# Spreading 1/rms with a stride-zero column, weight halves by accumulating transfers, twenty fills and new transfer constants in the planner

## The chip, the cores and the metric

One Trainium2 chip, one of its cores. The metric is the device time of one execution in microseconds (us). A core has five engines that run beside each other and wait for each other by semaphores: TensorE (PE, with its weight loads as PEld), VectorE (DVE), ScalarE (ACT), GpSimd (POOL) and SyncE (SP, which here only issues transfers). Each engine works through its own list of instructions strictly in the order in which the program put them there.

## The reference, cut to what matters

Two layers; `x` are 256 latent tokens, `xc` 256 context tokens, 1024 wide, everything in float32. The second layer leaves out the context's later part.

```python
for l in range(2):
    mod = silu(c) @ w_ada[l] + b_ada[l]        # nine vectors: shift, scale, gate, three times
    x = x + 0.5*g1 * swiglu(modulate(rmsnorm(x), sh1, sc1), w1, w3, w2)      # ffn 1, also for xc
    h = modulate(rmsnorm(x), sh2, sc2)
    # mixer: h @ w_in gives q, k, v, g of a retention with 8 heads, the low-rank
    # parts of an attention with 8 heads, and two merge gates
    ret = (silu(g) * groupnorm(retention(q, k, v))) @ w_ret_out
    x = x + g2 * ((sigmoid(gate_ret)*ret + sigmoid(gate_mla)*mla) @ w_o)
    x = x + 0.5*g3 * swiglu(modulate(rmsnorm(x), sh3, sc3), w1, w3, w2)      # ffn 2
return rmsnorm(x, final_norm)
```

`rmsnorm(x)` divides each token by the root of its mean square over the 1024 columns.

## The kernel before

**Layout.** Activations lie transposed: partitions are columns of the model, the free dimension is tokens (512 = 256 latent + 256 context), so x is eight tiles of 128x512. A weight tile of 128x1024 (512 KB) holds eight 128x128 blocks.

**Products in two halves.** TensorE multiplies the rounded type float32r in one pass. A float32 operand a is split into hi = round(a) and lo = a - hi, and a product is three matmuls, hi*hi + lo*hi + hi*lo (`mm3`, line 600). For weights `split_w` (line 562) does it: ACT copies `raw` to `wh`, then DVE subtracts to make `wl`. Transfers land in four `raw` buffers; `wh` and `wl` have four each.

**Norm** (lines 622 to 676). `add` squares a tile on ACT and sums on DVE; `stats` sums over partitions with a matmul against ones, which leaves the mean square of token p in partition p; DVE scales it and POOL takes the power -1/2, giving `rstd` with one column for each 128 tokens. `spread` brings this to a row on every partition: DVE multiplies the identity by each column of rstd (`dg`), and a float32 matmul of ones with dg gives 128x256. There are 19 of these: two each for start, n1, n2, n3 and the two low-rank norms of layer 0, and seven in layer 1.

**Stages.** `start` (line 1482) loads x, takes the first norm, computes the first shift and scale tile by tile (five on TensorE, three on DVE) and the first three pairs of ffn tiles as they arrive. It has 20 warm-up matmuls of ones with ones and `N_KEEP` = 5 more ("fills") of low priority. Then for each layer ffn 1, mixer, ffn 2. An ffn goes in three parts of 6, 8 and 8 hidden tiles: `up` makes a hidden tile G (ACT Silu, three DVE operations in `gate_tile`, line 855), `down` multiplies a part's tiles by w2. Between these, `ada_fill` puts the products for later shifts, scales and gates: DVE multiplies a `raw` tile of w_ada with a row into `junk` and sums it (line 726). In the mixer, eight steps `g_step` (line 1117) with one weight tile each go in turn with the retention's steps.

**Who sets the order.** All operations are recorded first. `Plan.order` (line 249) then simulates them: each engine takes, when free, the ready operation of lowest priority number; costs of operations come from `Engine.cost` (line 403). A transfer on SP costs 475 ns of the issuing engine, and lands at the later of its issue + 1100 ns and the one before it, plus bytes at 400 bytes/ns. The order found there is what each engine's list holds; on the chip nothing is reordered. All recorded instructions carry line 368.

Of the kernel before, what the change touches and what calls it, by code (L numbers as in the profile page):

```python
# [14 lines left out]
AF = mybir.ActivationFunctionType  # L15
# [3 lines left out]
P = 128  # L19
# [21 lines left out]
N_TAIL = 3  # L41
N_WARM = 20
N_PE_ADA = 5
N_KEEP = 5
URGENT = 1000
N_FIRST = 2
N_RQ = (1,3)
# [112 lines left out]
class Node:  # L160


    __slots__ = ("calls", "engine", "cost", "table", "port", "prio", "index", "waits", "after", "bufs", "new", "ready", "start", "end")

    def __init__(self, engine, prio, index):
        self.engine, self.prio, self.index = engine, prio, index
        self.calls, self.cost, self.table, self.port = [], 0.0, None, False
        self.waits, self.after, self.bufs, self.new = set(), [], {}, []
        self.ready, self.start, self.end = 0.0, None, None


class Plan:
# [7 lines left out]
    LONG, FAR, HOLD = 500.0, 1000, HOLD  # L180

    COLD = 7000.0

    def __init__(self, tc):
        self.tc = tc
# [63 lines left out]
    def order(self):  # L249
# [14 lines left out]
        later = {e: [] for e in engines}  # L264
        avail = {e: [] for e in engines}
        stuck = {k: [] for k in self.kinds}
        dma, table, port = 0.0, None, 0.0
        for n in nodes:
            if not left[n]:
                heapq.heappush(later[n.engine], (0.0, n.index, n))  # L270
# [17 lines left out]
        while len(done) < len(nodes):  # L288
# [34 lines left out]
                due[b.kind].remove(b.first)  # L323
            n.start = now
            if e == "SP":
                clock[e] = now + 475.0
                n.end = dma = max(now + 1100.0, dma) + n.cost
            else:
                if n.table not in (None, table):
                    now, table = now + self.TABLE, n.table  # L330
                if n.port:

                    now = max(now, port)
                    port = now + n.cost
                slow = 2.0 if e == "PE" and now < self.COLD else 1.0
                n.end = clock[e] = now + slow * n.cost
# [35 lines left out]
class Engine:  # L372
# [5 lines left out]
    def __getattr__(self, method):  # L378
        call = getattr(self.real, method)

        def record(*args, **kwargs):
            views = [v for v in list(args) + list(kwargs.values()) if isinstance(v, View)]
            out = [v for k in ("out", "accum_out") if isinstance(v := kwargs.get(k), View)]
            if "out" not in kwargs and args and isinstance(args[0], View):
                out.append(args[0])
            reads = [v for v in views if not any(v is o for o in out)]

            table = {AF.Silu: 0, AF.Exp: 1, AF.Tanh: 1}.get(args[2]) if method == "activation" else None
            return self.plan.add(self.name, call, args, kwargs, out, reads, self.cost(method, out, reads, kwargs), table,
                                 self.port(method, out, reads, kwargs))  # L390

        return record

    def port(self, method, out, reads, kwargs):

        if self.name == "POOL":
            return method != "memset"
        if self.name != "DVE" or any(v.buf.kind in ("m", "a") for v in out + reads):
            return False
        big = [v for v in reads if math.prod(v.shape[1:]) > 1]  # L400
        return len(big) > 1 or (method in ("tensor_copy", "tensor_scalar") and math.prod(out[0].shape[1:]) > 8)

    def cost(self, method, out, reads, kwargs):
# [3 lines left out]
        psum = any(v.buf.kind in ("m", "a") for v in out + reads)  # L407
        pointers = sum(isinstance(kwargs.get(k), View) for k in ("bias", "scale", "scalar", "scalar1", "scalar2"))
        if self.name == "SP":
            return big.shape[0] * n * 4 / 400.0  # L410
        if self.name == "PE":
            rows, cols = out[0].shape[0], math.prod(out[0].shape[1:])
            if method == "transpose":
# [8 lines left out]
        if self.name == "ACT":  # L422
            return 0.834 * n + (50.0 if psum else 93.0) + 91.0 * pointers + (96.0 if "accum_out" in kwargs else 0.0)
        if self.name == "POOL":
            if kwargs.get("op") == ALU.pow:
                return 300.0 + 165.0 * n
            if method == "memset":
                return 60.0 + 0.78 * n
            return (300.0 + 0.93 * n if method == "tensor_scalar" else 130.0 + 2.13 * n)
# [7 lines left out]
def kernel(  # L437
# [124 lines left out]
    def split_w(raw, n, kind):  # L562
        if kind == "raw":
            return raw
        if kind == "t":
            hi, lo = Halves(T(dt=F32R), T(dt=F32R)), Halves(T(dt=F32R), T(dt=F32R))
            for i in range(2):
                r = raw[:, i * TOK:(i + 1) * TOK]
                act.copy(out=hi.parts[i], in_=r)
                dve.tensor_tensor(out=lo.parts[i], in0=r, in1=hi.parts[i], op=ALU.subtract)  # L570
        else:
            hi, lo = plan.new("wh", n, F32R), plan.new("wl", n, F32R)
            act.copy(out=hi, in_=raw)
            dve.tensor_tensor(out=lo, in0=raw, in1=hi, op=ALU.subtract)
        return Pair(hi, lo)

    def run_steps():
# [44 lines left out]
    class Norm:  # L622
# [39 lines left out]
        def spread(self, a, n):  # L662

            rstd = self.ms.pop(a)
            dg = U(n)
            for i in range(n // P):
                dve.tensor_scalar(out=dg[:, i * P:(i + 1) * P], in0=ident, scalar1=rstd[:, i:i + 1], scalar2=None, op0=ALU.mult)
            bc = self.bc[a] = PA(n)
            pe.matmul(bc, lhsT=ones, rhs=dg, start=True, stop=True)

        def finish(self, a, n=LAT):
            if a not in self.bc:
# [280 lines left out]
    def mixer(l, nrm_in, nrm_out, full):  # L953
# [485 lines left out]
        for i in range(8):  # L1439
            if i % 2 == 0:  # L1440
                step(ret_state(i // 2))
                step(ret_scores(i // 2))
                if i >= 2:
                    step(ret_out(i // 2 - 1))
            step(g_step(i), W("g", i))
            if i % 2 == 0:
                step(ret_av(i // 2))
                if i < 6:
# [288 lines left out]
```

## Time and profile before

| | |
|---|---|
| three timed runs | median 2145.7 us (2140.36 to 2147.9) |
| the profiled execution | 2144.34 us, its span 2142.6 us |
| mean granted TensorE clock | 0.991 |
| instructions | 29830 |
| data read from HBM | 290.78 MB, 136 GB/s over the span |

The span runs from the first to the last instruction; some 1.7 us of the execution lie around it. The busy time of an engine is the union of its instructions. Matmuls are pipelined and their ends are modelled, so a stretch in which TensorE counts as busy can still hold short waits; a wait shows as idle time in brackets before an instruction, with who ended it.

### The profile page before, as it was taken

What the parts mean: (1) busy time and instruction counts of PE and PEld (TensorE: products, weight loads), DVE (VectorE), ACT (ScalarE), POOL (GpSimd) and SP (SyncE); (2) the same over time, 40 slices, a digit from 0 to 9 for tenths busy, and PEclk for the clock granted to TensorE, in tenths of its full rate; (3) what the DMA queues carried; (4) which work ended last, traced back from release to release, by engine and by line L of the source; (5) the groups of instructions that cost most, each with busy time, mean ns of one, the idle gap of its engine ahead of it and who ended that gap; (6) DMA issues with size and microseconds to landing.
All of it is one profiled execution on the core that took longest, in us unless ns stands there. A gap on an engine that the chain in (4) does not pass through costs nothing.

```text
span 2142.6 us, 29830 instructions
## 1 busy us (share of the span) xinstructions
PE 2112.4 (99%) x11630; PEld 1800.7 (84%) x11630; DVE 1402.9 (65%) x2599; ACT 745.1 (35%) x1225; POOL 150.6 (7%) x172
## 2 busy tenths in 40 slices
PE   9999999999999999999999999999999999999998
PEld 6888788987788888988878898888889879999998
DVE  6898785668679435888755473433337967766665
ACT  4222122476433223422212242221225744344433
POOL 0000000211132000100000010000002112100000
PEclk8999999999999999999999999999999999999999
DMA  8476564221121433466665432333233312474663
GB/s 315 148 219 190 181 189 141 91 84 60 60 70 60 128 112 104 138 199 212 189 187 175 139 119 70 109 97 97 90 98 95 116 60 88 149 264 142 205 187 109
DMA packets 87070, 293.76 MB, mean 137 GB/s; under 512 B 9617, under 2 KB 12817, under 8 KB 86929
## 3 DMA queue, kind: packets, MB, share of 16 engines
q1 hardware_dynamic: 86930, 291.87, 43.6%
q8 instruction: 91, 1.49, 0.3%
q14 instruction: 49, 0.40, 0.1%
HBM read 290.78 MB, written 1.05 MB: 136 GB/s over the span
## 4 chain that ended last, share of the span: by engine, by line
PE 71%; DVE 11%; issue 8%; DMA 7%; POOL 1%; ACT 0%; SPq 0%; POOLq 0%; DVEq 0%; ACTq 0%
PE m L368 66%; DMA raw<-in_w_ada_dram 5%; PE a L368 5%; DVE junk L368 5%; DVE t L368 3%; DVE wl L368 2%; DMA t<-in_w_ada_dram 1%; DVE s L368 1%; DVE u L368 1%; POOL s L368 0%; DMA wh<-in_w_ada_dram 0%; POOL t L368 0%; DVE x L368 0%; ACT t L368 0%; DMA raw<-in_w3a_dram 0%
## 5 line engine op out<-in xcount | busy, mean ns | idle before, releaser
L368 PE MATMUL m<-t,wh 128*128 128x512 f32 (+1 forms) x6248 | 1646.8, 351 | 12.2 <-DVE t L368 11.8
L368 PEld LDWEIGHTS m<-t,wh 128*128 128x128 f32 x6248 | 1092.8, 189 | 180.7 <-DVE t L368 14.9
L368 PE MATMUL m<-t,wl 128*128 128x512 f32 (+1 forms) x3124 | 1086.0, 349 | 0.0
L368 ACT CAST wh<-raw 128x1024 fp32r<-128x1024 f32 (+1 forms) x398 | 409.2, 1029 | 959.3 <-PE m L368 824.6
L368 PEld LDWEIGHTS m<-t,wl 128*128 128x128 f32 x3124 | 589.3, 189 | 82.4
L368 DVE TENSOR_TENSOR wl<-raw,wh 128x1024 fp32r<-128x1024 f32 (+1 forms) x398 | 476.5, 1198 | 259.6 <-ACT wh L368 258.6
L368 DVE SCALAR_TENSOR_TENSOR junk<-raw,crow 128x1024 f32<-128x1024 f32 x220 | 268.8, 1222 | 109.9 <-DMA raw<-in_w_ada_dram 106.6
L368 DVE SCALAR_TENSOR_TENSOR x<-m,mod,x 128x256 f32<-128x256 f32 x192 | 86.3, 479 | 124.4 <-PE m L368 124.1
L368 ACT ACTIVATE t<-m 128x512 f32<-128x512 f32 (+1 forms) x155 | 79.3, 513 | 248.1 <-PE m L368 244.0
L368 DVE TENSOR_TENSOR t<-t,t 128x512 fp32r<-128x512 f32 (+7 forms) x252 | 145.4, 585 | 5.0 <-ACT t L368 2.4
L368 DVE TENSOR_TENSOR t<-t,m 128x512 f32<-128x512 f32 (+1 forms) x91 | 54.3, 597 | 109.2 <-PE m L368 103.7
L368 POOL TENSOR_TENSOR s<-s,mhalf 128x2 f32<-128x2 f32 (+1 forms) x31 | 35.5, 1149 | 1163.4 <-DVE s L368 1163.2
L368 PE MATMUL m<-wh,t 128*128 128x512 f32 x288 | 92.1, 399 | 0.0
L368 PE MATMUL a<-t,t 128*64 128x256 f32 (+3 forms) x512 | 87.2, 351 | 4.8 <-DVE t L368 2.8
L368 PEld LDWEIGHTS a<-t,t 128*128 128x128 f32 (+1 forms) x512 | 66.0, 175 | 22.3 <-ACT t L368 4.9
L368 PE MATMUL m<-t,t 128*128 128x256 f32 (+1 forms) x480 | 76.0, 310 | 0.3 <-DVE t L368 0.3
L368 PEld LDWEIGHTS m<-t,t 128*128 128x128 f32 x480 | 65.2, 191 | 5.5 <-issue 1.2
L368 PEld LDWEIGHTS m<-wh,t 128*128 128x128 f32 x288 | 53.2, 188 | 12.6 <-issue 1.2
L368 ACT CAST t<-t 128x512 fp32r<-128x512 f32 (+4 forms) x112 | 55.9, 526 | 11.5 <-DVE t L368 8.9
L368 PE MATMUL m<-wl,t 128*128 128x512 f32 x144 | 56.9, 395 | 0.0
L368 ACT ACTIVATE t<-u,mod 128x256 fp32r<-128x256 f32 x88 | 39.7, 500 | 28.8 <-DVE u L368 28.8
L368 POOL MEMSET t<- 32x512 f32 x32 | 16.1, 528 | 473.7 <-DVE junk L368 257.3
(105 smaller groups left out, 1045.7 us busy)
## 6 DMA issues: line engine op xcount, KB each, us to landing
raw<-in_w_ada_dram SPq DMA_DIRECT2D x122, 512.0 KB, 4.2
raw<-in_w_m_dram SPq DMA_DIRECT2D x76, 512.0 KB, 3.5
raw<-in_w1b_dram SPq DMA_DIRECT2D x44, 512.0 KB, 3.9
raw<-in_w3b_dram SPq DMA_DIRECT2D x44, 512.0 KB, 3.8
raw<-in_w1a_dram SPq DMA_DIRECT2D x41, 512.0 KB, 3.6
raw<-in_w3a_dram SPq DMA_DIRECT2D x41, 512.0 KB, 3.6
raw<-in_w2a_dram SPq DMA_DIRECT2D x32, 512.0 KB, 3.5
raw<-in_w2b_dram SPq DMA_DIRECT2D x32, 512.0 KB, 3.6
```

Of the source, the lines that this page charges most:

```text
L368: call(*[resolve(v) for v in args], **{k: resolve(v) for k, v in kwargs.items()})
```

## The change

Four edits. `spread` takes the column of rstd itself, read 128 times with stride zero, as the stationary operand, and the identity as the moving one: row m of the result is the sum over k of rstd[k] * ident[k, n], so rstd[n] on all partitions. The multiplications on DVE are gone; there is a matmul for each 128 tokens. For the eight `g` weight tiles of each layer the lower half is made by ACT writing -raw (rounded, so -hi) into `wl` and a transfer issued by POOL that adds raw to it. N_KEEP goes from 5 to 20. The planner's constants for transfers change, and it learns to place transfers on POOL.

```diff
-N_KEEP = 5
+N_KEEP = 20
...
+    FIRST, ISSUE, LATENCY, RATE = 2000.0, 560.0, 2000.0, 380.0
...
-        dma, table, port = 0.0, None, 0.0
+        dma, table, port = self.FIRST, None, 0.0
...
             if e == "SP":
-                clock[e] = now + 475.0
-                n.end = dma = max(now + 1100.0, dma) + n.cost
+                clock[e] = now + self.ISSUE
+                n.end = dma = max(now + self.LATENCY, dma) + n.cost
+            elif n.moved:
+
+                clock[e] = now + n.cost
+                dma = max(now + self.LATENCY, dma) + n.moved
+                n.end = dma + 1800.0
...
+            if self.name == "POOL" and method == "dma_start":
+                node.moved += 1.5 * out[0].shape[0] * math.prod(out[0].shape[1:]) * 4 / 270.0
...
-            return method != "memset"
+            return method not in ("memset", "dma_start")
...
-            return big.shape[0] * n * 4 / 400.0
+            return big.shape[0] * n * 4 / Plan.RATE
...
+            if method == "dma_start":
+                return 870.0
...
             act.copy(out=hi, in_=raw)
-            dve.tensor_tensor(out=lo, in0=raw, in1=hi, op=ALU.subtract)
+            if kind == "d":
+
+                act.activation(lo, raw, AF.Copy, scale=-1.0)
+                pool.dma_start(out=lo, in_=raw, accum_op=ALU.add)
+            else:
+                dve.tensor_tensor(out=lo, in0=raw, in1=hi, op=ALU.subtract)
...
             rstd = self.ms.pop(a)
-            dg = U(n)
-            for i in range(n // P):
-                dve.tensor_scalar(out=dg[:, i * P:(i + 1) * P], in0=ident, scalar1=rstd[:, i:i + 1], scalar2=None, op0=ALU.mult)
             bc = self.bc[a] = PA(n)
-            pe.matmul(bc, lhsT=ones, rhs=dg, start=True, stop=True)
+            with plan.together():
+                for i in range(n // P):
+                    pe.matmul(bc[:, i * P:(i + 1) * P], lhsT=rstd[:, i:i + 1].to_broadcast([P, P]), rhs=ident, start=True,
+                              stop=True)
...
-            step(g_step(i), W("g", i))
+            step(g_step(i), W("g", i, "d"))
```

## Rows read from the trace of the kernel before

**Rows 1.** Page, part 1: busy us (share of the span) and instructions of each engine.

```profile
PE 2112.4 (99%) x11630; PEld 1800.7 (84%) x11630; DVE 1402.9 (65%) x2599; ACT 745.1 (35%) x1225; POOL 150.6 (7%) x172
```

**Rows 2.** Windows: length, busy us of PE, PEld, DVE, ACT, POOL, clock, DMA share, GB/s.

```profile
228.00:240.00 12.00, 7.31 (x22) 5.07 (x21) 9.34 (x15) 1.05 (x1) 0.00 (x0) 0.72 0.61 194
1080.00:1092.00 12.00, 9.71 (x34) 7.14 (x34) 7.61 (x15) 1.45 (x2) 0.00 (x0) 0.86 0.72 217
1812.00:1836.00 24.00, 18.20 (x126) 17.03 (x125) 21.27 (x55) 9.31 (x20) 5.88 (x7) 0.86 0.22 67
```

**Rows 3.** Timeline at 226 to 234 us: start, us, what, idle before.

```profile
226.45 1.46 SPq L368 DMA_DIRECT2D raw<-in_w_ada_dram  x2
...
229.90 1.23 DVE L368 SCALAR_TENSOR_TENSOR junk<-raw,crow 128x1024 f32<-128x1024 f32 x1 [1.98 <-DMA raw<-in_w_ada_dram]
...
231.05 0.68 DVE L368 TENSOR_TENSOR t<-t,m 128x512 f32<-128x512 f32 x1
...
233.25 0.79 PE L368 MATMUL m<-t,wh 128*128 128x512 f32 x1 [4.17 <-DVE t L368]
```

**Rows 4.** Timeline of DVE before 1080 us.

```profile
1078.82 1.23 DVE L368 SCALAR_TENSOR_TENSOR junk<-raw,crow 128x1024 f32<-128x1024 f32 x1 [3.14 <-DMA raw<-in_w_ada_dram]
```

**Rows 5.** Waits of DVE: us in total, times, longest.

```profile
DVE junk L368 <- DMA raw<-in_w_ada_dram: 106.6, 57, 4.0
```

**Rows 6.** Page, part 6: issues, KB each, us to landing.

```profile
raw<-in_w_ada_dram SPq DMA_DIRECT2D x122, 512.0 KB, 4.2
raw<-in_w_m_dram SPq DMA_DIRECT2D x76, 512.0 KB, 3.5
```

**Rows 7.** Windows, same columns: layer 1's retention.

```profile
1800.00:1812.00 12.00, 12.00 (x106) 12.00 (x105) 11.39 (x33) 7.25 (x16) 5.77 (x7) 1.00 0.18 68
```

**Rows 8.** Timeline of DVE and PE in layer 1's retention.

```profile
1766.27 1.22 DVE L368 TENSOR_TENSOR wl<-raw,wh 128x1024 fp32r<-128x1024 f32 x1 [5.09 <-ACT wh L368]
...
1812.87 1.23 DVE L368 TENSOR_TENSOR wl<-raw,wh 128x1024 fp32r<-128x1024 f32 x1
1814.01 0.41 DVE L368 SCALAR_TENSOR_TENSOR t<-t,m 128x256 f32<-128x256 f32 x1
...
1814.48 0.39 PE L368 MATMUL m<-t,wh 128*128 128x256 f32 x1 [1.45 <-DVE t L368]
```

**Rows 9.** Timeline at the last norm, 2134 to 2137 us.

```profile
2134.27 0.69 POOL L368 TENSOR_TENSOR s<-s,mhalf 128x2 f32<-128x2 f32 x1 [184.76 <-DVE s L368]
2135.00 0.48 DVE L368 TENSOR_SCALAR u<-ident,s 128x128 f32<-128x128 f32 x2 [0.81 <-POOL s L368]
...
2135.63 0.69 PE L368 MATMUL a<-u,ones 128*128 128x256 f32 x2 [1.64 <-DVE u L368]
```

**Rows 10.** Timeline from 888 to 899 us: the norm ahead of ffn 2, layer 0.

```profile
888.41 1.61 POOL L368 TENSOR_TENSOR s<-s,mhalf 128x2 f32<-128x2 f32 x1 [0.43 <-DVE s L368]
...
890.05 0.95 DVE L368 TENSOR_SCALAR u<-ident,s 128x128 f32<-128x128 f32 x2 [0.19 <-POOL s L368]
...
898.06 0.38 PE L368 MATMUL m<-t,wh 128*128 128x256 f32 x1 [2.10 <-DVE t L368]
```

**Rows 11.** Timeline of PE at 1815 us: float32 matmuls of 128 columns.

```profile
1815.52 1.05 PE L368 MATMUL a<-t,t 128*128 128x128 f32 x8
```

**Rows 12.** Timeline of PEld and PE in the start.

```profile
49.84 0.42 PEld L368 LDWEIGHTS a<-ones 128*128 128x128 f32 x2
...
63.17 2.60 PE L368 MATMUL m<-t,t 128*128 128x512 f32 x10 [0.32 <-DVE t L368]
```

**Rows 13.** Groups by form: busy us, mean ns, idle before.

```profile
L368 DVE TENSOR_TENSOR wl<-raw,wh 128x1024 fp32r<-128x1024 f32 x360 | 440.1, 1224 | 246.3 <-ACT wh L368 245.3 <-PE m L368 0.3
L368 ACT CAST wh<-raw 128x1024 fp32r<-128x1024 f32 x360 | 377.5, 1050 | 867.1 <-PE m L368 746.1 <-issue 101.6 <-DVE junk L368 6.1
```

**Rows 14.** Windows, same columns: the start.

```profile
13.00:30.00 17.00, 17.00 (x78) 9.39 (x77) 8.03 (x22) 7.53 (x17) 0.94 (x2) 0.50 1.02 359
...
37.00:63.00 26.00, 25.85 (x117) 21.00 (x117) 26.00 (x58) 10.84 (x20) 0.00 (x0) 1.00 0.43 172
```

More of the change, by code (lines that the diff above doesn't have):

```diff
@@ L160 @@
 class Node:
-    __slots__ = ("calls", "engine", "cost", "table", "port", "prio", "index", "waits", "after", "bufs", "new", "ready", "start", "end")
+    __slots__ = ("calls", "engine", "cost", "table", "port", "moved", "prio", "index", "waits", "after", "bufs", "new", "ready", "start", "end")
     def __init__(self, engine, prio, index):
         self.engine, self.prio, self.index = engine, prio, index
-        self.calls, self.cost, self.table, self.port = [], 0.0, None, False
+        self.calls, self.cost, self.table, self.port, self.moved = [], 0.0, None, False, 0.0
         self.waits, self.after, self.bufs, self.new = set(), [], {}, []
@@ L388, in record @@
             table = {AF.Silu: 0, AF.Exp: 1, AF.Tanh: 1}.get(args[2]) if method == "activation" else None
-            return self.plan.add(self.name, call, args, kwargs, out, reads, self.cost(method, out, reads, kwargs), table,
+            node = self.plan.add(self.name, call, args, kwargs, out, reads, self.cost(method, out, reads, kwargs), table,
                                  self.port(method, out, reads, kwargs))
+            if self.name == "POOL" and method == "dma_start":
+                node.moved += 1.5 * out[0].shape[0] * math.prod(out[0].shape[1:]) * 4 / 270.0
+            return node
         return record
```

## The prediction

> **What bounds the kernel now.** First the page's busy times: TensorE is busy for 2112.4 us of 2142.6, every other engine for 65% or less [rows 1]. So the end is set by TensorE's list plus the places where it stands still (30 us in all), and a removed instruction of DVE is worth something only where it stands ahead of such a place. Second, the windows around the places where the timeline shows TensorE waiting, with their clock [rows 2]. At 228 to 240 us it is busy for 7.31 of 12 us and the granted clock is 0.72. The clock has two levels (1.2 and 2.4 GHz), so 0.72 means 0.28 x 2 x 12 = 6.7 us at the lower one, entered after the standstill. Of the 4.7 idle us I take half to lie in it; the other 4.4 us are work at half speed, 2.2 us lost. That place costs 4.7 + 2.2 = 6.9 us. The same sum at 1080 to 1092: 2.3 idle, 3.4 us slow, all working: 4.0 us. At 1812 to 1836: 5.8 idle, 6.7 us slow with about 5 working: 8.3 us. Third, what ended those waits.
>
> At 233.25 TensorE has waited 4.17 us for a hidden tile that DVE makes; DVE began that tile's product with PSUM only at 231.05, because ahead of it in its list stood a `junk` product that sat idle for 1.98 us until its load from w_ada landed [rows 3]. The load was issued from 226.45 on. At 1078.82 the same: DVE idle 3.14 us for such a load, with the hidden tile behind it [rows 4]. Over the run DVE waits 57 times, 106.6 us, for these loads [rows 5]; at most places nobody is behind it. The planner put them there: by its constants one 512 KB load lands 1100 ns + 524288/400 = 2.41 us after issue, where the page has 4.2 and 3.5 us [rows 6]. In layer 1's retention it is DVE's own load: busy 11.39 of 12 us ahead of the standstill [rows 7], and the wait at 1814.48 ends right after a `wl` of 1.23 us and a 0.41 us product [rows 8].
>
> **The change part by part.**
>
> *Spread.* 19 times it removes two DVE instructions (0.48 us for the pair at the end) and one handover. Where nothing else runs, the power ends at 134.27 + 0.69 = 134.96 (last three digits of the time) and the matmul starts at 135.63, 0.67 us later [rows 9]. POOL can release TensorE directly; I take 0.15 us for that handover, about what lies between dg's end (135.48) and the matmul. Gain 0.5 us, at the end and at the norm ahead of ffn 2 in layer 1, which has the same chain. Ahead of ffn 2 in layer 0 the pair took 0.95 us on a DVE that TensorE then waits 2.10 us for [rows 10]; 0.6 of it counts. The other 16 lie beside other matmuls: nothing, while TensorE has some. Sum -1.6. On TensorE a float32 matmul of 256 columns (two instructions, 0.69 us with its drain [rows 9]) becomes two of 128 columns, four instructions; eight such take 1.05 us with the drain [rows 11], so four about 0.45 against 0.42. That is +0.03 x 19 = +0.5 us. The trace shows no weight load with stride zero: as cheap as any other gives +0.5; four unhidden loads of 0.21 (half of 0.42 for two [rows 12]) each time, +16; below nothing only the two loads saved if reading one column is free, -8. I take +0.5, the value of the nearest rows, plain loads and matmuls of that size. Net -1.1.
>
> *The planner's constants.* A load now lands 2.0 + 524288/380 ns = 3.38 us after issue in its books, close to the 3.5 of w_m. A load issued at 226.45 would be expected at 229.8 instead of 228.9, against the real use at 229.90. With the hidden tile's product ready earlier in its books, it would go first, and its four DVE steps would be done before TensorE runs dry. I give each of the two places two chances in three: -(6.9 + 4.0) x 2/3 = -7.3. But the whole order is found anew, and 57 waits get other neighbours: one new place with a chance of one half, at the mean price of the two, 5.45: +2.7. Net -4.6. Its ends: -10.9 (both go, none comes) and +16.6 (five such places, the second rival below).
>
> *Lower halves by transfer.* In each layer eight `wl` of 1.22 us leave DVE, and ACT gets eight more of about 1.05 [rows 13]. In layer 1 the eight stand between 1766.27 and 1812.87 [rows 8], the last of them directly ahead of the product that TensorE waits for. DVE is full from 1800 at the latest; the last two, 2.4 us, lie there, and without the six before, 7.3 us, it enters that stretch with less backlog. Of the 8.3 us I count 5; nothing in layer 0, where I read no standstill at this step that matters. ACT is busy 7.25 of 12 us there [rows 7], so 1.05 more for each tile fits, with 0.5 us of delays. The transfer itself is not in the trace. Nearest row: a load of the same bytes, 3.5 us [rows 6]; it reads two streams and writes one, so up to three times that, 10.5. With four `wl` buffers a tile can be made three ahead of its use, and eight took 46.6 us from first to last, 6.7 each: a lead of some 15 to 20 us, so either end is hidden, as are the 2.0 + 2.9 + 1.8 us that the planner now books for it. What POOL spends on issuing is not in the trace; the nearest rows are its power of two columns, 0.69 us alone [rows 9] and 1.61 beside a busy DVE [rows 10]; from nothing to 1.61 us each, then. POOL is busy 5.77 of 12 us there; 0.5 us for a power that stands behind an issue. Net -5.0 + 1.0 = -4.0, with ends -8.3 and +5 (ACT's 8 x 1.05 and half of POOL's 8 x 1.61 in the chain, 14.8, less the 9.8 of DVE).
>
> The Trainium skill has a rule against this: "SBUF — State Buffer", section "SBUF: two separate sides", says that a transfer issued from GpSimd needs descriptors written by its cores, which are locked out while DVE runs a two-port copy. No row of before has such a transfer, so no trace here shows it yet; only the power's 1.61 us against 0.69 points that way. By the page's own case (about 620 ns growing to about 3100) the estimate would be a transfer that starts 2.5 us later, which the lead above hides; what it would do to POOL's own list is the third rival, worked out from rows.
>
> *Fills.* 15 more, two instructions of 128 columns each, 0.22 us at full clock by [rows 11]. Three of the old five lie at 49 to 51 us, in a TensorE without gaps [rows 12]. All 15 there cost 3.3 us, less the 0.32 that TensorE then waits at 63.17 anyway. In the gaps of 8 to 25 us they cost nothing and may keep the clock up, which is 0.50 from 13 to 30 us [rows 14]. That is 17 us at half speed, but transfers are then at a share of 1.02 of their engines, and from 37 to 63 DVE is busy 26.00 of 26: what a faster TensorE can give is only DVE work moved ahead into the 9.0 us that DVE is idle from 13 to 30, of which I allow a third, 3.0. Ends -3.0 and +3.0; I take -0.5, nearer to the gaps since the new constants make the planner see TensorE idle there. The start's order is also new; it lies within the same ends.
>
> *Sum:* -1.1 - 4.6 - 4.0 - 0.5 = -10.2 us. Against the profiled execution: 2144.3 - 10.2 = 2134.1. That execution was 1.4 us below the median of the runs, 2145.7, so I forecast 2135.5 us for a median.
>
> **Rivals.**
>
> *The standstills only move.* A new order removes one and makes another, and the retention's DVE stays full because ACT and POOL now hold the chain. For: 57 waits, two of which hurt, is a matter of neighbours. Against: expected landings get nearer to real ones, and an order from better numbers runs dry less. Then only the spread's 1.1 and a third of the transfers' 4.0 are left: 2145.7 - 2.4 = 2143.
>
> *Part ends run dry more often (slower).* Place: the end of an ffn's part, where `down` needs the last hidden tile, and its four DVE steps stand behind a `junk` product or a `wl`. There are twelve such places; two ran dry. Price: 5.5 us each with the slow clock behind, the mean of 6.9 and 4.0. For: with 15 fills and loads thought later, the planner may hold products back to those ends. Against: later landings in its books put the tile first, not the load. Beside the other parts' gains of 5.6 us it decides from three places on (16.4 instead of 10.9 takes them up), and five make 27.5 - 10.9 - 5.6 = +11: 2157.
>
> *POOL held up by its transfers.* POOL issues eight in a layer, in order with the powers on which the group norm's DVE steps wait, four of them in layer 1. The planner books 870 ns for an issue; made longer as the power was, by 1.61/0.69, it is 2.0 us, and one ahead of each of four powers in a stretch where TensorE runs dry is 8 us: 2135.5 + 8 = 2144. For: the slow power. Against: POOL is idle for half of that stretch [rows 7]. The section of the Trainium skill named above speaks for this one.
>
> *All of it pays.* Both places gone (-10.9), all 8.3 of the retention, spread -1.1, start -3.0: -23.3, so 2122.
>
> **How the numbers follow.** Forecast 0.42 (its own range 2128 to 2141), only moved 0.20, part ends 0.17, POOL 0.05, all pays 0.16. A difference of 0.3%, 6.4 us, is about what the measurement can tell: below 2139.3 is faster, above 2152.1 slower. Faster: 0.16 + 0.40 of the forecast's 0.42 = 0.56. Slower: the part ends' 0.17, where three places stay within the bound and five do not, less 0.03 for the former, + 0.04 for sizes at their bad ends under any case = 0.18. Same: the rest, 0.26, mostly the rivals that only move things. The range 2121 to 2152 leaves out about 0.04 below and 0.16 above.
>
> **What would show it.** Right: no `dg` on DVE and 76 float32 matmul instructions of 128 columns in their place; the norm at the end 0.5 us shorter; DVE's waits for w_ada well below 106.6 us; TensorE without the waits at 233 and 1082 us and with the clock at 1.00 there; layer 1's retention with less than 3 idle us; 382 `wl` on DVE. Wrong: weight loads of the spread above 0.3 us; waits of over 2 us of TensorE at other part ends; powers on POOL that wait behind transfers; fills in a row inside 30 to 63 us.

## The result and the profile after

The changed kernel takes 2122.58 us (median of four runs, 2122.4 to 2123.7), the kernel before 2146.16 beside it (2140.36 to 2147.9): a ratio of 0.9896, 95% interval 0.9877 to 0.9915. That is 23.6 us, or 1.0%, faster. The forecast was 2135.5, so 10.2 us: the sign was right, the size was less than half of it. Its profiled execution took 2123.70 us, with a span of 2121.9: 20.7 us less than the profiled one before.

Page, part 1, of the changed kernel (against [rows 1]):

```profile
PE 2104.7 (99%) x11698; PEld 1801.8 (85%) x11698; DVE 1379.2 (65%) x2545; ACT 759.8 (36%) x1241; POOL 160.6 (8%) x188
```

TensorE's idle time went from 30.2 us (2142.6 - 2112.4) to 17.2, and its busy time fell by 7.7 although it has more instructions: work that ran at the lower clock now runs at the higher. The windows of the changed kernel around the three places of [rows 2], in the same columns:

```profile
216.00:228.00 12.00, 12.00 (x53) 9.68 (x53) 10.13 (x20) 2.11 (x2) 0.00 (x0) 1.00 0.58 180
1064.00:1076.00 12.00, 12.00 (x53) 9.74 (x52) 8.29 (x14) 2.09 (x2) 0.00 (x0) 1.00 0.65 204
1789.00:1813.00 24.00, 21.13 (x165) 20.34 (x165) 22.59 (x60) 10.90 (x22) 8.01 (x10) 0.93 0.36 105
```

The first two standstills are gone, clock and all; the third is halved (2.9 us idle instead of 5.8). At the first of them the timeline of the changed kernel (start, us, what, idle before) stands against [rows 3]:

```profile
216.08 1.46 SPq L375 DMA_DIRECT2D raw<-in_w_ada_dram  x2
...
219.28 0.69 DVE L375 TENSOR_TENSOR t<-t,m 128x512 f32<-128x512 f32 x1 [1.73 <-PE m L375]
220.00 0.43 DVE L375 CAST t<-t 128x512 fp32r<-128x512 f32 x1
220.37 1.23 DVE L375 TENSOR_TENSOR wl<-raw,wh 128x1024 fp32r<-128x1024 f32 x1
...
222.11 1.22 DVE L375 SCALAR_TENSOR_TENSOR junk<-raw,crow 128x1024 f32<-128x1024 f32 x1
```

The load is issued as before, but in DVE's list the hidden tile's product (`t<-t,m`) now stands ahead of the `junk` product. DVE waits for TensorE there, and not TensorE, by way of DVE, for a load. The load's 1.98 us were only a part of the 4.17 us that TensorE waited: in the kernel before, DVE had to get through the `junk` product itself (1.15 us to the next instruction) and through a `wl` (1.13) between the tile's product and its rounding, too. The timeline of the kernel before, behind the tile's product of 231.05:

```profile
231.65 1.22 DVE L368 TENSOR_TENSOR wl<-raw,wh 128x1024 fp32r<-128x1024 f32 x1
232.78 0.42 DVE L368 CAST t<-t 128x512 fp32r<-128x512 f32 x1
```

In the changed kernel both stand behind the rounding (`CAST`).

**Where the 20.7 us went.** TensorE's products with `wl` come in the same number (3124) and nearly the same order in all these kernels, so the n-th of them marks the same place. The table gives, for stretches between such marks, the change of the time from mark to mark against the kernel before, in us, from the start times in the traces ("alone": the kernel before with that one edit). Each column is one profiled execution.

| stretch of before (us) | whole | constants alone | fills alone | spread alone | transfers alone |
|---|---|---|---|---|---|
| start, to 67 | -4.0 | -1.8 | +2.7 | -0.8 | -0.3 |
| 207 to 242, first standstill | -7.2 | -7.3 | +0.6 | +2.7 | +0.7 |
| 453 to 550, attention of layer 0 | -1.5 | 0.0 | 0.0 | -1.6 | 0.0 |
| 550 to 691, retention of layer 0 | +1.1 | 0.0 | -0.1 | -0.1 | +1.1 |
| 876 to 900, norm ahead of ffn 2 | -2.3 | -0.8 | +1.1 | -2.3 | 0.0 |
| 1069 to 1101, second standstill | -4.4 | -4.4 | +2.8 | +1.2 | +1.6 |
| 1670 to 1795, attention of layer 1 | +1.1 | 0.0 | 0.0 | +1.3 | 0.0 |
| 1795 to 1862, retention of layer 1 | -3.0 | 0.0 | -0.1 | +0.4 | -4.2 |

The rows left out come to about -0.5 in the whole. Where a standstill remains, its row differs by up to 2.8 us between kernels of which none touches it, so the positive numbers of the other edits in those two rows say little about the edits. The constants account for at least 11.6 of the 20.7.

### The profile page after: what moved, and what is told of

The parts are those of the page before. It is cut to its first block, busy times and chain, and to the rows that moved or that the text cites. A ratio compares the mean times of both kernels' runs of the same rounds, so it can differ in the third digit from the quotient of the medians.

```text
span 2121.9 us, 29994 instructions
## 1 busy us (share of the span) xinstructions
PE 2104.7 (99%) x11698; PEld 1801.8 (85%) x11698; DVE 1379.2 (65%) x2545; ACT 759.8 (36%) x1241; POOL 160.6 (8%) x188
## 4 chain that ended last, share of the span: by engine, by line
PE 94%; DVE 4%; issue 1%; POOL 1%; ACT 1%; DMA 0%; POOLq 0%; DVEq 0%; ACTq 0%
PE m L375 87%; PE a L375 7%; DVE t L375 2%; DVE u L375 1%; DVE wl L375 1%; DVE s L375 0%; POOL t L375 0%; ACT wh L375 0%; POOL s L375 0%; DMA raw<-in_w3b_dram 0%; ACT t L375 0%; DVE x L375 0%; ACT wl L375 0%; POOLq L1749 0%; ACT u L375 0%
## 5 line engine op out<-in xcount | busy, mean ns | idle before, releaser
L375 DVE TENSOR_TENSOR wl<-raw,wh 128x1024 fp32r<-128x1024 f32 (+1 forms) x382 | 457.4, 1199 | 249.6 <-ACT wh L375 248.8
L375 POOL TENSOR_TENSOR s<-s,mhalf 128x2 f32<-128x2 f32 (+1 forms) x31 | 30.7, 995 | 1173.6 <-DVE s L375 1173.5
```

The source lines that it names most:

```text
L375: call(*[resolve(v) for v in args], **{k: resolve(v) for k, v in kwargs.items()})
```

## The experiments

**Each edit alone**, on the kernel before. The four diffs, cut to their cores:

```diff
+    FIRST, ISSUE, LATENCY, RATE = 2000.0, 560.0, 2000.0, 380.0      # constants
...
-N_KEEP = 5
+N_KEEP = 20                                                         # fills
...
+    pe.matmul(bc[:, ...], lhsT=rstd[:, i:i + 1].to_broadcast([P, P]), rhs=ident, ...)   # spread
...
+    step(g_step(i), W("g", i, "d"))                                 # transfers
```

Constants: 

> The kernel before with the planner's new transfer constants alone (spread by DVE, five fills, all lower halves by DVE). Theory A (the constants cure the standstills where DVE waits for a load ahead of a hidden tile): the lost 7.2 us at 206 to 242 us and the 4.4 us at 1069 to 1101 us are gone, the start is about as before, in all about -12 us, 2134 us. Theory B (any new order dissolves a standstill and makes others; the gain of the whole change is spread over the edits): about -6 us, 2140 us, and one of the two standstills stays or a new one of over 2 us comes. Theory C (the fills give most of the start's 4 us): the start is within 1 us of before.

Fills: 

> The kernel before with 20 fills alone. Theory A: only the start moves; with theory C it is 2 to 4 us shorter and the clock is back at its upper level before 20 us instead of 30; both standstills (at 229 and 1081 us) stay; in all 2143 us. Rival (fills only cost TensorE time in the start, the 4 us come from the constants): the start 1 to 3 us longer, 2148 us. Theory B: the two standstills move or go here as well.

Spread: 

> The kernel before with the spread by the stride-zero column alone. Theory A: both standstills stay; the stretch ahead of ffn 2 of layer 0 (876 to 900 us) is 2 us shorter, the start 0 to 1 us shorter, the end the same to 0.5 us; 2143 us. Theory B: other stretches move by over 2 us too, the two standstills among them.

Transfers: 

> The kernel before with the lower halves of g by transfers alone (old constants for SP's loads; the planner books the POOL transfers by its new rule with the old 1100 ns). Theory A: nothing moves before layer 0's retention, both standstills stay; layer 1's retention 2 us shorter (the prediction had counted 5, and 4 net); 2143 us. Theory B: the two standstills or others move. If POOL held the chain: layer 1's retention longer than before, 2148 us or more.

| alone | median us (range) | ratio to before (2148.13) | 95% |
|---|---|---|---|
| constants | 2128.34 (2127.5 to 2128.83) | 0.9916 | 0.9894 to 0.9939 |
| fills | 2151.14 (2145.1 to 2154.11) | 1.0014 | 1.0000 to 1.0027 |
| spread | 2143.86 (2140.88 to 2146.98) | 0.9984 | 0.9968 to 1.0001 |
| transfers | 2143.24 (2130.13 to 2146.52) | 0.9980 | 0.9962 to 0.9998 |

The constants alone remove both standstills and bring no other: 19.8 us between the medians, 16.3 between the profiles. That is theory A, with 1.8 us from the start and 0.8 at the norm ahead of ffn 2 besides. The scatter is smaller too: the 25 runs of the kernel before beside them lay between 2136.63 and 2153.7, the four of this one within 1.3 us. The three others leave both standstills in place. The fills alone cost 2.7 us in the start, as the rival had it: they stand in a row at 49 to 53 us, in a TensorE without gaps. In the time of the whole kernel the intervals of the fills and the spread reach to 1 (no change), and that of the transfers nearly does, so what these three are worth is read from the stretches that they touch.

**Is it the landing time?** First the one constant that says when a load lands, alone; then all new constants with that one too early:

```diff
+    FIRST, ISSUE, LATENCY, RATE = 0.0, 475.0, 2000.0, 400.0       # the landing time only
...
+    FIRST, ISSUE, LATENCY, RATE = 2000.0, 560.0, 500.0, 380.0     # new, but landing at 500 ns
```

> The kernel before with one constant changed: a load is booked to land 2000 ns after its issue at the earliest instead of 1100; issue, rate and first transfer stay at 475, 400 and 0. Theory A (both standstills went because the hidden tile's product is now put ahead of the junk product that waits for a load, so the landing time alone is enough): TensorE runs through 230 and 1081 us, -7.3 - 4.4 = -11.7 us against the kernel before, and its runs scatter less. Theory B (it needs the slower rate and issue too, or it is chance that the new order misses these places): one or both standstills stay, less than 8 us gained.

> The kernel before with the new constants except the landing time, which is booked at 500 ns instead of the new 2000 (before: 1100). Theory A (what counts is that the booked landing is as late as the real one, 3.5 to 4.2 us for 512 KB): the standstills at 230 and 1081 us stay or grow, as loads are thought earlier than before; time 2140 or more. Theory B (any other order would miss those two places, they were bad luck): both gone, about 2129, as with the constants alone.

The landing time only: 2131.44 us (2129.67 to 2132.22), ratio 0.9933 (0.9920 to 0.9947), both standstills gone (-7.2 and -4.4 by the marks). At 500 ns: 2178.78 us (2178.45 to 2183.23), ratio 1.0160 (1.0141 to 1.0178), 32 us slower. That is theory A in both, and stronger than expected at 500 ns. A later run took the other side, 4000 ns alone:

```diff
+    FIRST, ISSUE, LATENCY, RATE = 2000.0, 560.0, 4000.0, 380.0
```

> The kernel before with the new constants but a landing time of 4000 ns (500 gave 2178.8, 1100 about 2146, 2000 gave 2128.3). Theory A (only being too early costs; both standstills stay away): 2127 to 2132. Theory B (a landing booked too late holds products back to the parts' ends, as the second rival said of the new constants): above 2135, with new places where TensorE waits for a hidden tile.

2136.13 us (2134.86 to 2137.89), ratio 0.9959 (0.9945 to 0.9973). The waits of these kernels (engine, line, what it waited for: us in total, times, longest), first the kernel before, whose wait of DVE for loads is in [rows 5]:

```profile
PE m L368 <- DVE t L368: 12.1, 8, 4.2
```

Landing booked at 500 ns:

```profile
DVE junk L375 <- DMA raw<-in_w_ada_dram: 174.2, 75, 4.5
...
PE m L375 <- DVE t L375: 34.8, 13, 11.9
```

The landing time only (2000 ns, the other constants old):

```profile
DVE junk L375 <- DMA raw<-in_w_ada_dram: 55.5, 36, 3.7
...
PE m L375 <- DVE t L375: 4.3, 4, 1.4
```

Constants alone (2000 ns):

```profile
DVE junk L375 <- DMA raw<-in_w_ada_dram: 50.6, 34, 3.7
...
PE m L375 <- DVE t L375: 4.6, 4, 1.4
```

At 4000 ns:

```profile
DVE junk L375 <- DMA raw<-in_w_ada_dram: 0.7, 2, 0.4
...
PE m L375 <- ACT t L375: 4.4, 5, 2.4
PE m L375 <- DVE t L375: 3.4, 3, 1.4
```

Read as a series, 500, 1100 (before, whose other constants are the old ones; the landing time alone shows how little these matter here), 2000 and 4000 ns: DVE waits 174.2, 106.6, 50.6 and 0.7 us for the loads, and TensorE 34.8, 12.1, 4.6 and 3.4 us for a tile that DVE makes. Of these last, the waits for a hidden tile at the end of an ffn's part are 29.5, 7.0, 0 and 0 us; the rest lie in layer 1's retention, at the norm ahead of ffn 2 and in the start. The waits of DVE go on falling, but TensorE's for hidden tiles are gone by 2000 ns: the loads that DVE still waits for then have nobody urgent behind them. And 4000 costs 7.8 us against 2000: by the marks 4.4 in the start and 2.7 at the norm ahead of ffn 2 of layer 0. At the norm TensorE waits 2.38 us for ACT, where with the constants alone it waits 1.09 us for DVE; why ACT is later, and the start, was not followed up. So booking late costs as well, though not at the parts' ends: neither theory as I had written it. What an early landing does is seen in the timeline of the 500 ns kernel, DVE and TensorE at 240 us:

```profile
240.60 1.23 DVE L375 SCALAR_TENSOR_TENSOR junk<-raw,crow 128x1024 f32<-128x1024 f32 x1 [2.64 <-DMA raw<-in_w_ada_dram]
...
241.87 1.23 DVE L375 SCALAR_TENSOR_TENSOR junk<-raw,crow 128x1024 f32<-128x1024 f32 x1
...
243.02 0.68 DVE L375 TENSOR_TENSOR t<-t,m 128x512 f32<-128x512 f32 x1
...
245.23 0.79 PE L375 MATMUL m<-t,wh 128*128 128x512 f32 x1 [9.96 <-DVE t L375]
```

Two `junk` products stand ahead of the hidden tile, the first of them waiting for its load, and TensorE is idle for 9.96 us.

In the whole change the same constant was moved once more:

```diff
-    FIRST, ISSUE, LATENCY, RATE = 2000.0, 560.0, 2000.0, 380.0
+    FIRST, ISSUE, LATENCY, RATE = 2000.0, 560.0, 3000.0, 380.0
```

> The changed kernel with its loads booked to land at 3000 ns at the earliest instead of 2000 (with the rate that is 4.4 us for 512 KB, above the real 3.5 to 4.2). Theory A (once the booked landing is about the real one nothing is left to gain): 2122.6 within 2 us, the start's order decides the sign. Theory B (the later the better): the remaining waits for loads of DVE, 47.5 us, fall again and the time by 2 us or more.

2123.82 us (2121.06 to 2125.02), ratio 0.9896 (0.9880 to 0.9912). DVE's waits for loads fell to 10.2 us, and the time stayed: theory A.

**The fills.** With 5 and with 11 in the whole change (N_KEEP alone is edited):

> The changed kernel with 5 fills instead of 20. In the start (first matmul of the first ffn, 62.96 us in the changed kernel) the whole change gained 4.0 us, the four edits alone sum to -0.2. Theory A (the gain needs the fills and the new constants together: eleven of the fills land in the gap at 18 to 22 us and keep the granted clock up, which returns at 17.7 us instead of 30.1): without them the start loses at least 2.2 us, the time is 2124.8 to 2127. Theory B (the fills only cost, nine of them standing in TensorE without gaps at 44 to 50 us at 0.2 us each; the constants with the transfers or the spread gave the start): about 1.8 us faster, 2120.8. Either way no standstill near 230 and 1081 us.

> The changed kernel with 11 fills, so that if the order stays the same the eleven in the gap at 18 to 22 us stay and the nine at 44 to 50 us go. Theory A (fills pay in the gap and cost 0.2 us each where TensorE has no gap): 9 x 0.2 = 1.85 us faster, 2120.7. Theory B (the fills' place does not matter because DVE, busy from 37 to 63 us, sets the end of the start): no change, 2122.6 within 0.7.

With 5: 2125.64 us (2122.96 to 2125.85), ratio 0.9904 (0.9889 to 0.9919). With 11: 2126.77 (2123.2 to 2131.04), ratio 0.9912 (0.9895 to 0.9929). By the medians five are 3 us worse than twenty, as theory A had it; eleven are 4 us worse, which neither theory had. (By the marks the start of the first is 2.4 us longer than with twenty, that of the second 4.7.) But a number of fills also changes the order of the start. So the next two keep the order that the planner finds with twenty, and only leave fills out of what is issued (n is 11, then 0):

```diff
-            for _ in range(N_KEEP):
-                pe.matmul(fill, lhsT=ones, rhs=ones, start=True, stop=True)
+            for i in range(N_KEEP):
+                node = pe.matmul(fill, lhsT=ones, rhs=ones, start=True, stop=True)
+                if i >= n:
+                    node.calls.clear()
```

> The changed kernel in exactly its own order, with the last 9 of its 20 fills (those at 44.5 to 50.4 us, in a TensorE without gaps) not issued; everything else on every engine's list is the same. Theory A (each costs its own 0.2 us and gives nothing): 9 x 0.2 = 1.8 us earlier at the first ffn, about 2120.8. Theory B (DVE, without idle time from 36 to 63 us, sets when the first ffn starts, so TensorE's fills there are hidden): no change, 2122.6 within 0.5.

> The changed kernel in exactly its own order, with none of its 20 fills issued, so that the order that the planner found with 20 fills is kept and only their work and what it does to the clock goes. Theory A (the fills themselves pay: they keep the granted clock up in the start): later by 2 to 4 us than the changed kernel, 2124.6 to 2126.6, with the clock at half speed for longer than its 3.41 us. Theory B (the order found with 20 fills pays, not the fills: 3 us against the whole with 5, 4 against the whole with 11): 2122.6 or below, by up to 1.8 us.

Without the late nine: 2123.36 us (2122.47 to 2123.74), ratio 0.9898 (0.9883 to 0.9913): no gain (0.8 above the changed kernel, which the scatter covers), so theory B rather than A. Without any: 2122.18 (2120.06 to 2125.6), ratio 0.9895 (0.9879 to 0.9912): the same median with 5.5 us of scatter instead of 1.3. The start's windows of the changed kernel (against [rows 14]), then of the one without the late nine, then without any:

```profile
13.00:30.00 17.00, 17.00 (x129) 11.36 (x129) 9.60 (x27) 9.03 (x22) 1.40 (x2) 0.90 1.05 388
37.00:63.00 26.00, 26.00 (x124) 21.61 (x124) 26.00 (x53) 11.39 (x19) 0.00 (x0) 1.00 0.49 185
```

```profile
37.00:63.00 26.00, 24.93 (x106) 19.48 (x105) 26.00 (x55) 10.79 (x18) 0.00 (x0) 1.00 0.47 173
```

```profile
13.00:30.00 17.00, 16.48 (x103) 9.38 (x103) 9.33 (x26) 9.07 (x22) 0.82 (x2) 0.70 1.06 395
37.00:63.00 26.00, 24.98 (x106) 19.46 (x105) 26.00 (x53) 11.19 (x19) 0.00 (x0) 1.00 0.47 177
```

From 37 to 63 us DVE is busy all the time with and without the fills, and taking the late nine away leaves TensorE 1.07 us idle: DVE sets the end of the start, and these fills lie beside it. From 13 to 30 us the clock is 0.90 with the fills and 0.70 without, which cost nothing in that execution (the first ffn starts 3.9 us earlier than before instead of 4.0): by this pair it is the order, theory B.

**Transfers and spread taken out of the whole:**

```diff
-            step(g_step(i), W("g", i, "d"))
+            step(g_step(i), W("g", i))
```

> The changed kernel with the lower halves of the output gate's weights on DVE again. Theory A (the terms add up: the transfers alone gave 4.2 us between 1795 and 1862, in the whole 3.0 less the 1.1 that it loses at 1670 to 1795): 2.5 to 4 us slower, 2125 to 2126.6, layer 1's retention with its 8.3 us place back. Theory B (with the new constants the place is eased by the order anyway): within 1 us of 2122.6.

2126.03 us (2124.9 to 2126.58), ratio 0.9911 (0.9896 to 0.9925): 3.5 us slower than the changed kernel by the medians, theory A. But these runs were not made beside the changed kernel's, the intervals of the two ratios overlap, and the two profiled executions are only 1.2 us apart (2124.90 and 2123.70). By the marks of these two, leaving the transfers out loses 2.2 us in layer 1's retention, and gives back 1.1 in layer 0's and 0.4 in the start. Layer 1's retention, 1790 to 1814 us, without the transfers and then with them:

```profile
1790.00:1814.00 24.00, 18.37 (x140) 17.21 (x138) 23.13 (x59) 10.39 (x21) 7.58 (x10) 0.89 0.18 49
```

```profile
1790.00:1814.00 24.00, 21.13 (x161) 20.34 (x160) 22.08 (x59) 10.27 (x21) 7.01 (x9) 0.91 0.32 90
```

2.8 us more of TensorE's work in the same 24 us. What is left of the standstill stands in the timeline of the changed kernel:

```profile
1807.87 0.93 PE L375 MATMUL a<-t,t 128*128 128x256 f32 x4 [1.10 <-DVE t L375]
...
1808.87 1.23 DVE L375 TENSOR_TENSOR wl<-raw,wh 128x1024 fp32r<-128x1024 f32 x1
1810.01 0.41 DVE L375 SCALAR_TENSOR_TENSOR t<-t,m 128x256 f32<-128x256 f32 x1
...
1810.48 0.58 PE L375 MATMUL m<-t,wh 128*128 128x256 f32 x1 [1.68 <-DVE t L375]
```

It is the same pattern as in [rows 8]: a `wl` of 1.23 us, of another weight than the output gate's eight, ahead of the product that TensorE waits for.

The spread by DVE again, in the whole (the old `spread` of the diff):

> The changed kernel with the spread by DVE again. Theory A (the pair of DVE instructions was on the path wherever TensorE waits for a norm in a stretch without other work: 2.0 us in latent attention of layer 0 at 453 to 496, 1.5 us beyond the constants' 0.8 at the norm ahead of ffn 2): 2 to 3.5 us slower, 2124.6 to 2126.1. Theory B (as the prediction had it: 0.5 us at three norms less 0.5 us of matmuls): 1.1 us slower, 2123.7.

2124.37 us (2121.33 to 2125.15), ratio 0.9901 (0.9886 to 0.9916): 1.8 us slower by the medians, between the two theories. But its runs overlap with the changed kernel's, and the two profiled executions are 0.07 us apart, so that what the spread is worth in the whole, 0 to 1.8 us, isn't told by this. By the marks it loses 1.5 us in layer 0's attention and 1.3 at the norm ahead of ffn 2, and gets 1.1 back in the start (-5.1 against -4.0) and 1.1 in layer 1's attention. That last one is a wait of TensorE, in the timeline of the changed kernel and then of this one:

```profile
1674.10 2.82 PE L375 MATMUL a<-t,t 128*128 128x512 f32 x11 [1.28 <-DVE t L375]
```

```profile
1675.10 2.82 PE L375 MATMUL a<-t,t 128*128 128x512 f32 x11 [0.38 <-DVE t L375]
```

**Transfers in layer 1 alone**, and the same without issuing the fills (as above, n = 0):

```diff
-            step(g_step(i), W("g", i, "d"))
+            step(g_step(i), W("g", i, "d" if l else "w"))
```

> The changed kernel with the transfers in layer 1 alone; layer 0's eight lower halves are on DVE again. The whole loses 1.05 us at 549 to 691 us (layer 0's retention), the kernel with the transfers alone 1.1 at the same place. Theory A (the transfers put layer 0's chain on ACT and POOL later and give nothing there): 1 us faster than the changed kernel, 2121.5, with layer 1 as it is. Theory B (the loss there is the order's, or comes back before the next ffn): no change, 2122.6 within 0.5.

> The same with the 20 fills planned but not issued: the best that the runs point to. Theory A: as the kernel with the transfers in layer 1 alone, and by what the fills showed in the changed kernel's order (0.4 us between the medians) no more than 0.5 below it, 2121. Theory B (with another order in the start the fills matter): over 1 us away from it, to either side.

In layer 1 alone: 2120.82 us (2120.24 to 2121.73), ratio 0.9887 (0.9871 to 0.9902). The +1.1 of layer 0's retention is gone (0.0 by the marks), theory A. In the changed kernel a part of it is this wait in the timeline of TensorE:

```profile
611.48 2.35 PE L375 MATMUL a<-t,t 128*128 128x256 f32 x16 [1.05 <-DVE t L375]
```

Without layer 0's transfers a wait of 0.83 us at 638.74 us stands in its place, and TensorE is idle for 0.8 us in that retention instead of 1.5. That is 0.6 of the 1.1 us; the rest lies in time in which TensorE counts as busy, and its cause is not shown.

All five runs lie below the changed kernel's four. They were not run beside each other, and the intervals of the ratios overlap, so 1.8 us is what the medians say and no more.

Without its fills the same kernel takes 2124.88 us (2121.04 to 2125.53), ratio 0.9899 (0.9882 to 0.9915): 4.1 slower, theory B. The start's window, first with the fills, then without:

```profile
0.00:37.00 37.00, 35.62 (x235) 27.17 (x236) 21.53 (x59) 21.05 (x50) 2.53 (x11) 0.95 0.96 345
```

```profile
0.00:37.00 37.00, 35.10 (x197) 24.13 (x198) 17.98 (x51) 19.94 (x49) 2.53 (x11) 0.77 0.97 346
```

The clock is 0.77 where it was 0.95, and DVE has done 17.98 us of work by 37 us instead of 21.53. It has no idle time from there to 63, so these 3.55 us come back at the first ffn (-0.9 by the marks instead of -4.3). So in this pair the fills pay. The two pairs do not agree: by the medians, leaving the fills out changed nothing in the changed kernel and cost 4.1 us here. The window up to 37 us of the former, without its fills:

```profile
0.00:37.00 37.00, 35.10 (x211) 25.09 (x212) 20.89 (x58) 20.27 (x49) 2.54 (x11) 0.86 0.98 353
```

There the clock fell less, and DVE lost little. Each of the two kernels without fills has runs at both ends: 2120.06 us at a mean clock of 0.997 and 2125.6 at 0.994 in the one, 2121.04 and 2121.38 at 0.996 and four from 2124.55 to 2125.53 at 0.992 to 0.995 in the other. With twenty fills the runs of each kernel lie within 1.3 and 1.5 us, and the clock is 0.95 up to 37 us in both profiles. I read this as a clock that falls for longer in some executions than in others when the fills are missing; that it is the clock of the start that differs is not shown for the runs without a profile. The fills are then worth 0 to 4 us, by the execution. With eleven fills and an order of their own it is another matter:

```profile
0.00:37.00 37.00, 35.08 (x208) 23.30 (x208) 17.32 (x49) 18.46 (x45) 2.57 (x11) 0.91 0.96 347
```

The clock is 0.91, but DVE has done only 17.32 us of work. What the clock does not explain lies in the order, and why that order is worse was not followed up.

## Why the prediction was wrong

**What bounds the kernel: right.** The three places of [rows 2] gave 14.6 of the 20.7 us, for the reasons read from [rows 3, 4, 8].

**The constants, -4.6 instead of -11.6 at these places (-16.3 by the profiles of the constants alone): the step that failed.** The two places were priced at 6.9 and 4.0 us and measured 7.2 and 4.4. What failed was what was made of the price: "I give each of the two places two chances in three", and "one new place with a chance of one half ... +2.7". The argument ahead of it said that the tile goes first once the load is thought later; a mean over its chances was then entered as the likeliest time. The charge for new places had no reason of its own but that the order is found anew. The runs show that the new neighbours aren't drawn by chance: the nearer the booked landing comes to the real one, the less TensorE waits for hidden tiles, 29.5, 7.0 and 0 us. This is 7.0 of the 10.5 us between the span's change and the forecast. The other 3.5 are the start's. The spread and the transfers were put at -5.1 together, and all rows but the start and the two standstills come to -5.1 too; as the parts below show, that agreement is luck.

The booked landing could have been judged by the page alone: 2.41 us in the books against 3.5 and 4.2 on the chip [rows 6] is early, 3.38 is nearly right. The Trainium skill ("DMA: Bandwidth & Descriptors", section "Anatomy of one DMA — SWDGE (gpsimd) path") gives a fixed part of about 2.0 us for each transfer, for one that GpSimd issues; SP's loads here agree with it rather than with the old 1.1: 3.5 us less the 1.38 that the new rate books for the bytes is 2.1, an estimate. The transfers that GpSimd itself issues here add as well, and take 5.0 us.

**The start, -4.0 instead of -0.5: mis-sized.** Its bounds were -3.0 to +3.0, from a third of the idle 9.0 us of DVE. The mechanism was the one named, DVE work moved ahead into its gaps with 37 to 63 us full as before; but the gaps were counted from 13 to 30 us alone, and from 30 to 37 there were more. The window up to 37 us, first of the kernel before, then of the changed one:

```profile
0.00:37.00 37.00, 34.37 (x190) 23.49 (x191) 18.32 (x53) 19.02 (x46) 2.53 (x11) 0.77 0.95 336
```

```profile
0.00:37.00 37.00, 35.62 (x234) 27.39 (x235) 21.09 (x59) 20.12 (x50) 2.54 (x11) 0.95 0.96 349
```

DVE is 2.8 us ahead by then. That it has two `dg` pairs of the start less to do is not what gave it: with the spread by DVE again the first ffn starts 1.1 us earlier still. The fills alone cost 2.7 and the constants alone gave 1.8; only together do eleven of the fills stand in the gaps at 18 to 23 us. How much of the 4.0 is these fills and how much the order found with them stays open: without issuing them the start was 3.9 us shorter than before in one profile, 0.9 in the other. "Nearer to the gaps since the new constants make the planner see TensorE idle there" was the right reason with too small a number.

**The spread, -1.1: its size not told (0 to -1.8), its places wrong.** The matmuls cost no more than was said: the four take 0.61 us at the higher clock, the old two 0.69 [rows 9]. Ahead of ffn 2 in layer 0 the norm gave 1.3 instead of 0.6, at the end next to nothing. There, the timeline of the changed kernel (against [rows 9]):

```profile
2113.33 0.69 POOL L375 TENSOR_TENSOR s<-s,mhalf 128x2 f32<-128x2 f32 x1 [184.82 <-DVE s L375]
...
2114.08 1.22 PE L375 MATMUL a<-ident,s 128*128 128x128 f32 x4 [1.02 <-POOL s L375]
2115.33 0.37 ACT L375 COPY u<-a 128x256 f32<-128x256 f32 x1 [3.16 <-PE a L375]
```

The matmuls start 0.06 us after the power (0.15 was taken), but take 1.22 us; the same four at 876.75 us, at the higher clock, take 0.61. The clock, 0.65 from 2112 to 2117 us, fell in the wait for this norm, and the gain of 0.5 went there: ACT's copy starts 1.31 us after the power, in the kernel before 1.39 (at 2136.35). Where the clock holds, the gain is there. In the kernel with the transfers in layer 1 alone it is 1.00 from 2111 to 2112.5 us, and the copy starts 0.80 us after the power:

```profile
2110.77 0.70 POOL L375 TENSOR_TENSOR s<-s,mhalf 128x2 f32<-128x2 f32 x1 [184.86 <-DVE s L375]
...
2111.52 0.71 PE L375 MATMUL a<-ident,s 128*128 128x128 f32 x4 [1.03 <-POOL s L375]
2112.27 0.37 ACT L375 COPY u<-a 128x256 f32<-128x256 f32 x1 [2.66 <-PE a L375]
```

The larger gain was unforeseen: 1.5 us in layer 0's attention, costed at nothing as "beside other matmuls". The order there changed, and TensorE lost waits for ACT and DVE; that it was the two DVE instructions themselves is not shown. Layer 1's attention lost 1.1 by the same kind of shift.

**The transfers, -4.0: measured -3.5 by the medians and -1.2 by the profiles when left out, and not as worked out.** "Of the 8.3 us I count 5": 4.2 alone and 3.0 in the whole, with TensorE idle for 2.9 us in both; what differs is the mean clock of that stretch, 0.97 and 0.95. "Nothing in layer 0": +1.1. What POOL spends and when they land, in the list of issues of the changed kernel (KB each, median us to landing), beside an ordinary load:

```profile
raw<-in_w_m_dram SPq DMA_DIRECT2D x76, 512.0 KB, 3.6
...
wl<-raw POOLq DMA_DIRECT2D x16, 512.0 KB, 5.0
```

5.0 us lies well inside the bounds of 3.5 to 10.5. An issue takes POOL 850 to 1149 ns (median 884), within the bounds of nothing to 1.61 us. The rule of the Trainium skill ("SBUF — State Buffer", "SBUF: two separate sides") that DVE locks GpSimd's descriptors out did not show: the transfer issued at 575.49 us, with DVE idle until it landed, took 4.60 us, and the one at 610.96, with DVE busy all the time, 4.53. That rule speaks of two-port copies; whether DVE's work here is of that kind no run shows. The landings of the 16 lie between 4.4 and 7.9 us, and the nine slowest have ordinary loads beside them. The rival with POOL held up did not come in layer 1: an issue costs 0.88 us (median), not the 2.0 that it assumed. What cost 1.1 us in layer 0 is not shown.

**The rivals.** "All of it pays" gave 2122, and its sum is the one that came, though not by its parts: it had 8.3 us in the retention (3.0 measured), 3.0 in the start (4.0) and 1.1 for the spread (0 to 1.8). "Part ends run dry more often" needed three new places; there was none with the new constants. With a landing of 500 ns it happens, at three ends of parts and 32 us slower: the two old places grown, and a new one at 978 us with 3.0 us of waits. So the mechanism exists, and the sign of the constant's error decides.

## What to carry to other kernels

Where a planner's constant is compared with the measured duration of the thing that it stands for, the direction of its error tells the sign of a correction: a load booked as landing too early puts work that waits for it ahead of work that is ready, and each such place costs its wait and the lower clock behind it. Booked too late it costs as well, at other places. When the argument says that a cause goes, enter its full price as the likeliest value and keep the doubt for the range; a charge for "some new trouble" needs a mechanism too. Below the bound, an edit that removes instructions from an engine that is not the limit still moves the order, by about a microsecond to either side for each stage.

## What the runs showed of the hardware

- A stationary operand read with stride zero costs what any other does: the 76 weight loads of the spread have a median of 190 ns (185 to 338), the plain ones of `wh` a mean of 188.
- A transfer that adds within SBUF (512 KB) landed after 5.0 us (median of 16; 4.4 to 4.8 where next to no load ran beside it), loads of that size from HBM after 3.5 to 4.3 (medians by tensor).
- The scatter is mostly larger where standstills remain: the kernel before and the three single edits that keep both ran over ranges of 4 to 17 us, the changed kernel and the one with the constants alone over 1.3. It is not a sure sign: the kernel with eleven fills has neither standstill and ran over 7.8 us.
- A norm with nothing beside it can pay for the clock: the same four matmuls took 0.61 us at the higher clock and 1.22 at the end, where the clock had fallen.
